# A plan that holds its side steps: `HOLD` in the tracing order of a two-layer decoder step

## The chip, the cores and the metric

The kernel runs on one core of a Trainium2 chip. The metric is device time in microseconds (us) of one execution. Of the kernel before there are three runs: 3317.22, 3322.49 and 3330.22 us, median 3322.49.

## The reference

The reference is one inference step of a decoder trunk with two layers, for a prompt of 2048 tokens and for 8 sampled sequences of 8 tokens each (64 rows), with a model width of 1024. Every layer computes x + W_out(mixer(RMSNorm(x) W_in) * silu(gate)).

- Layer A is a gated DeltaNet with 8 heads of 128. q, k and v go through a causal convolution of width 4 and silu, q and k are normalised per head. Per chunk of tokens a unit lower triangular system is solved (a delta rule in its chunked form), and a state of 128 x 128 per head goes from chunk to chunk: `u = sol_v - sol_k S`, `o = e^G q S + (q k^T * decay) u`, `S' = e^G_last S + k^T u`.
- Layer B is a retention with 4 heads of 256 x 512, rotary positions and a decaying state: `o = (q k^T * D) v + q_dec * q S`, `S' = s_dec S + (k * k_dec)^T v`.

A last RMSNorm follows. Returned are the outputs for prompt and samples, and all states after the step. Everything is computed to float32 accuracy.

## The kernel before

The prompt is cut into four blocks of 512 tokens (`TB`); the 64 sample rows ride with one of the blocks, whose projections are then 576 wide. Layer A goes over the blocks n = 0 to 3 and in each over four groups of two heads (g = 0 to 3); then layer B goes over the blocks and its four heads.

*Projections.* A projection (`proj`, `colproj`, `colproj2`) multiplies a column tile of weights with the normalised block. Weights and activations are split into a high and a low part of type fp32r (`wload`, `split`), and three of the four products are taken (`PASSES`), so a column tile of 512 tokens is 8 x 3 = 24 products of 128 x 512. After each k, which is three products or six, the projection calls `pipe.pump()`. Per group of layer A there are eight such tiles: two of K, two of Z for the group before (`z_proj`), two of Q, two of V. `outproj_A` multiplies the outputs of a pair of groups with W_out.

*Side work.* All that is not a projection is written as Python generators, which `_Pipe` traces step by step in between. Per group of layer A these are

- `front_k` (prio 3): decay matrices, two steps of transposes of K (`tp`), and K K^T (`kp`) with its mask
- `front_x` (prio 2): the inverse of the triangular system. DVE substitutes within 32 x 32 pieces for a long time (`LAT_SUB`), with a way through DRAM before and behind; then PE joins the pieces in four steps of small products (`p1` to `p4`, in the trace `p`)
- `front_q` and `front_v` (prio 4): transposes of Q (`tq`), K Q^T (`kq`), transposes of V (`tv`)
- `chain` (prio 0): the recurrence over four chunks, three steps each (`kyd` and `o` in the trace; the copy `y` at L612 is in the middle of a chunk)
- a post per chunk (`gdn_post`, prio 1): transposes of the output (`oT`), the gate, and the split into `OG`

In blocks 1 and 2 a group of samples is added behind group 0: its fronts, and `chain_s` (prio 1), over four pairs of heads, with five `yield`s each (3.0, `LAT_C`, `LAT_C`, 1.0, 1.0). In layer B `ret_prompt` and `ret_sample` have prio 0, their posts prio 1, `colsum`, `final` and `final_s` prio 2. `gates` of layer A, once a block, has prio 0.

*What sets the order.* `_Pipe` keeps a clock of its own, `t`, which only PE's products advance: 0.4167 ns a column for fp32r, 1.667 ns a column for float32 but at least 0.11 us, 0.11 us a transpose (`mm`, `tr`). A task is runnable when its `deps` are done, and due when `ready <= t`. A step runs the generator to its next `yield`, whose value is the latency after which the task is due again, counted from the start of the step:

```
k.ready = self.t + next(k.gen)
```

`pump` runs all that is due, lowest prio first, until nothing is. `wait(task)` pumps until the task is done, and where nothing is due it moves the clock on to the next `ready`. A task that is added gets its `ready` at that moment, so one that has to wait for its `deps` is due at once when they are done. The latencies are the constants at the end (`LAT_T` 0.8, `LAT_K` 5.5, `LAT_SUB` 51, `LAT_M` 1.8, `LAT_Q` 0.7, `LAT_C` 2.0, `LAT_O` 4.3, `LAT_E` 4.0). The framework makes the queues of the engines from the traced order and inserts all semaphores; with `PIN = False` the traced order is a priority, and an instruction whose operands or buffers are not ready by its own reckoning can be passed by a later one.

*What waits for what.* `front_k` of a group waits for `front_q` of the group before; `front_q` waits for `front_k` and for the last chain added; `front_v` for `front_q`; a chain for `front_v`, `front_x` and the chain before it. The chain of samples stands in this line as well: `front_q` and the chain of group 1 wait for it. Group g begins with `pipe.wait` on the chain of group g - 2, its V projection waits for `front_v` of group g - 1, and `z_proj` for the chain before. `ring` gives the three `OG` buffers out; where the next one is still in use it calls `flush_A(0)`, which waits for the chains and posts of a pair and traces `outproj_A`. This falls on the end of V of group 0 (waiting for the last chain of the block before) and of group 2 (waiting for the chain of group 1) in blocks 1 and 2. Before layer B's V projection of its first head, `open_B` calls `finish_A`, which waits for the last chain and traces the last `outproj_A`.

Weights go through two raw buffers (`wraw`) and three split ones (`w`). PSUM has three banks for projections (`pp`), two for transposes and fronts (`f`), one for the chain (`c`), two for outputs (`o`). All loads and stores are issued by SP in one queue.

Of the kernel before, what the change touches and what calls it, by code (L numbers as in the profile page):

```python
# [35 lines left out]
class _Pipe:  # L36


    def __init__(self, tc):
        self.tc = tc  # L40
        self.t = 0.0
        self.tasks = []
# [17 lines left out]
            k.done = True  # L60
            self.tasks.remove(k)

    def pump(self):
        while True:
            c = [k for k in self._runnable() if k.ready <= self.t]
            if not c:
                return
            self._step(min(c, key=lambda k: (k.prio, k.ready)))

    def wait(self, *ks):  # L70
        for k in ks:
            while k is not None and not k.done:
                self.pump()
                if not k.done:
                    self.t = max(self.t, min(x.ready for x in self._runnable()))

# [11 lines left out]
def tile_hybrid(ctx: ExitStack, tc: tile.TileContext, a: dict, S: int):  # L88
# [7 lines left out]
    def mm(out, lhsT, rhs, start=True, stop=True):  # L96
        ins = nc.tensor.matmul(out, lhsT, rhs, start=start, stop=stop)  # L97
        n = rhs.free_size()
        pipe.t += (max(0.4167 * n, 107.0) if rhs.dtype == F32R else max(1.667 * n, 110.0)) / 1000.0
        if PIN:  # L100
            tc.keep_in_program_order(ins)
        return ins

    def tr(out, x):
        p = x.shape[0]
        ins = nc.tensor.transpose(out, x, ident[:p, :p])  # L106
        pipe.t += 0.11
        if PIN:
            tc.keep_in_program_order(ins)
# [412 lines left out]
    def front_q(x):  # L522
        QK, dec, Gb, kds = x.QK, x.dec, x.Gb, x.kds
        Am = pa.tile([128, 8, 128], F32, tag="Am", name="Am")
        Kd = x.Kd
        eq = pa.tile([128, 8], F32, tag="eq", bufs=2, name="eq")
        for q in range(2):
            tp = v3(pf("tq"), 128)
            for u in range(4):
                tr(tp[:, u, :], QK[:, 4 * q + u, 1, :])  # L530
            for u in range(4):
                ACT.activation(Am[:, 4 * q + u, :], tp[:, u, :], AF.Square, accum_out=eq[:, 4 * q + u : 4 * q + u + 1])
            yield LAT_T
        V.tensor_scalar(eq, eq, EPS, 128.0 * EPS, op0=ALU.add, op1=ALU.mult)
        for q in range(2):
            q4 = slice(4 * q, 4 * q + 4)
            kp = v3(pf("kq"), 128)
            for u in range(4):
                mm(kp[:, u], QK[:, 4 * q + u, 0, :], QK[:, 4 * q + u, 1, :])
            V.tensor_tensor(Am[:, q4], kp, dec[:, q4], op=ALU.mult)  # L540
            V.tensor_tensor(Kd[:, q4], Kd[:, q4], kds[:, q4].unsqueeze(2).to_broadcast([128, 4, 128]), op=ALU.mult)
            yield LAT_Q
            V.tensor_tensor(QK[:, q4, 1, :], QK[:, q4, 1, :], Gb[:, q4], op=ALU.mult)
        x.Am, x.eq = Am, eq

    def front_v(x, VTq):
        vn = pa.tile([128, 8, 128], F32, tag="vn", name="vn")
        for q in range(2):
            q4 = slice(4 * q, 4 * q + 4)
            VTu = VTq(q)  # L550
            if x.samp:
                yield 2.0
            tp = v3(pf("tv"), 128)
            for u in range(4):
                tr(tp[:, u, :], VTu(u))
            V.tensor_tensor(vn[:, q4], tp, x.nk[:, q4].unsqueeze(2).to_broadcast([128, 4, 128]), op=ALU.mult)
            yield LAT_T
        x.vn = vn
# [253 lines left out]
    def add_front(x, gt, nq, hsl, samp):  # L812
        x.fk = pipe.add(front_k(x, gt, nq, hsl, samp), 3, [x.g, last["fq"]], LAT_E, hp=HP_K)
        x.fx = pipe.add(front_x(x, samp), 2, [x.fk, last["fx"]], hp=HP_X)
        last["fx"] = x.fx

    def add_fq(x):
        x.fq = pipe.add(front_q(x), 4, [x.fk, last["ch"]], LAT_E, hp=HP_Q)
        last["fq"] = x.fq
# [47 lines left out]
    for n in range(NB):  # L867
# [22 lines left out]
        for g in range(4):  # L890
# [27 lines left out]
            for hh in range(2):  # L918
                pst = colproj(a["w_in_a"][16 + 2 * g + hh], xk, width)
                if g in (1, 2) and n + 1 < NB:  # L920
                    stats_A(n + 1, [2 * g - 2 + hh])
                    if g == 2 and hh == 1:
# [3 lines left out]
            x.fv = pipe.add(front_v(x, lambda q, VT=VT: lambda u: VT[:, u % 2, (2 * q + u // 2) * 128 : (2 * q + u // 2 + 1) * 128]),  # L926
                            4, [x.fq], LAT_E)
            if g == 3:
# [419 lines left out]


PIN = False  # L1350
LAT_E = 4.0
LAT_SUB = 51.0
LAT_K = 5.5
# [123 lines left out]
```

## Time and profile before

| | |
|---|---|
| median of three runs | 3322.49 us (3317.22 to 3330.22) |
| profiled execution | 3320.32 us, span 3318.5 us |
| granted TensorE clock, mean | 0.995 |
| PE busy | 97% (18847 instructions) |
| weight loads on PE (PEld) | 81% |
| DVE, ACT, POOL busy | 66%, 44%, 7% |
| chain that ended last | PE 83%, DVE 6%, DMA 4%, ACT 3% |

Busy times of PE are those of pipelined instructions: a product of 128 x 512 shows some 0.36 to 0.4 us, while in an unbroken run one starts every 0.23 us. So the distance from start to start tells what a stretch costs, and the busy share only where PE stood still. Layer A takes the time to about 1453 us, layer B the rest.

### The profile page before, as it was taken

The page shows a single profiled execution, that of the slowest core. Times are in us where ns is not written, and L with a number is a line of the kernel's source. Part 1 is how long each engine was busy: PE and PEld are TensorE (multiplying, and loading weights), DVE is VectorE, ACT ScalarE, POOL GpSimd, SP SyncE. Part 2 cuts the span into 40 slices and gives each one's busy share as a digit, 9 for nine tenths or more (in the row PEclk, how much of TensorE's full clock was granted, in tenths as well). Part 3 has the DMA queues.
Part 4 walks back from the last instruction along what each step waited for, and adds up shares of the span by engine and source line. Part 5 has one row for each costly group of instructions (what it writes and reads, how often), then busy time and mean ns, then how long its engine had stood idle before and what let it go on. Part 6 is the DMA issues. An engine that isn't in the chain of part 4 may idle for free.

```text
span 3318.5 us, 50681 instructions
## 1 busy us (share of the span) xinstructions
PE 3231.2 (97%) x18847; PEld 2700.4 (81%) x18847; DVE 2198.3 (66%) x4943; ACT 1453.5 (44%) x3243; POOL 240.2 (7%) x501
## 2 busy tenths in 40 slices
PE   7999999999999999999999999999999999999998
PEld 7999787778788888788888788877888788878886
DVE  6876778688878877755555665556564656575556
ACT  7655555465545645333333442343342433343333
POOL 1221011001110000000000000000000000000000
PEclk9999999999999999999999999999999999999999
DMA  4333454435444343552223442126232523253222
GB/s 134 96 101 85 144 167 142 132 106 152 130 129 126 89 143 99 151 162 82 74 82 106 129 163 89 59 83 194 77 116 82 171 68 116 71 175 117 89 77 70
DMA packets 241111, 379.78 MB, mean 114 GB/s; under 512 B 100688, under 2 KB 130144, under 8 KB 240864
## 3 DMA queue, kind: packets, MB, share of 16 engines
q1 hardware_dynamic: 240864, 376.54, 37.6%
q8 instruction: 148, 2.42, 0.3%
q14 instruction: 99, 0.81, 0.1%
HBM read 318.90 MB, written 55.46 MB: 113 GB/s over the span
## 4 chain that ended last, share of the span: by engine, by line
PE 83%; DVE 6%; DMA 4%; ACT 3%; POOL 1%; issue 1%; SPq 0%; DVEq 0%; POOLq 0%; ACTq 0%
PE pp L97 53%; PE pv L97 10%; PE o L97 5%; PE p L97 5%; PE kyd L97 2%; PE oT L106 1%; DMA st<-in_state_ret 1%; PE kp L97 1%; DVE w L182 1%; PE ap L97 1%; POOL so L572 1%; PE kq L97 1%; PE os L97 1%; ACT on L569 1%; PE pvs L97 1%
## 5 line engine op out<-in xcount | busy, mean ns | idle before, releaser
L97 PE MATMUL pp<-xn,w 128*128 128x512 f32 (+1 forms) x7760 | 1648.5, 362 | 13.2 <-ACT w L181 4.2
L97 PEld LDWEIGHTS pp<-xn,w 128*128 128x128 f32 x7760 | 1267.3, 189 | 210.2 <-issue 13.9
L181 ACT CAST w<-wraw 128x1024 fp32r<-128x1024 f32 x416 | 436.8, 1050 | 691.4 <-PE pp L97 449.0
L182 DVE TENSOR_TENSOR w<-wraw,w 128x1024 fp32r<-128x1024 f32 x416 | 508.4, 1222 | 249.1 <-ACT w L181 248.0
L97 PE MATMUL pp<-OG,w 128*128 128x512 f32 (+1 forms) x2880 | 582.6, 360 | 6.3 <-DVE xas L1167 3.2
L97 PEld LDWEIGHTS pp<-OG,w 128*128 128x128 f32 x2880 | 482.0, 190 | 89.8 <-issue 3.6
L97 PE MATMUL pv<-w,xn 128*128 128x512 f32 x1536 | 370.8, 396 | 0.0
L97 PEld LDWEIGHTS pv<-w,xn 128*128 128x128 f32 x1536 | 287.1, 188 | 73.8 <-issue 5.0
L1162 DVE TENSOR_TENSOR xa<-xa,pp 128x512 f32<-128x512 f32 (+2 forms) x160 | 90.2, 579 | 137.2 <-PE pp L97 137.1
L728 DVE SCALAR_TENSOR_TENSOR acc<-pp,cw,acc 128x511 f32<-128x511 f32 (+2 forms) x216 | 160.4, 742 | 22.0 <-ACT acc L725 21.7
L990 POOL TENSOR_TENSOR so<-oss,rsc 128x1 f32<-128x1 f32 x72 | 17.8, 247 | 1412.5 <-ACT on L988 1412.5
L981 DVE TENSOR_TENSOR rt<-pp,cs 128x512 f32<-128x512 f32 (+2 forms) x80 | 46.3, 578 | 105.9 <-PE pp L97 105.9
L473 DVE TENSOR_TENSOR VP<-VP,tm 128x66 f32<-128x66 f32 (+26 forms) x510 | 106.5, 209 | 4.4
L471 DVE TENSOR_TENSOR tm<-LP,VP 128x66 f32<-128x66 f32 (+26 forms) x510 | 104.3, 204 | 4.4
L97 PE MATMUL p<-Vt,Kt 128*128 128x512 f32 x384 | 104.4, 405 | 0.6 <-ACT on L992 0.6
L195 ACT CAST OG<-og 128x256 fp32r<-128x256 f32 x192 | 71.7, 405 | 62.0 <-DVE og L628 33.4
L97 PE MATMUL o<-Sc,Qc 128*128 128x512 f32 x360 | 93.4, 394 | 0.0
L196 DVE TENSOR_TENSOR OG<-og,OG 128x256 fp32r<-128x256 f32 x192 | 75.4, 420 | 20.8 <-ACT OG L195 20.5
L106 PE MATMUL oT<-ident,on 128*128 128x128 f32 x432 | 73.1, 276 | 11.4 <-DVE on L573 9.5
L97 PEld LDWEIGHTS p<-Vt,Kt 128*128 128x128 f32 x384 | 68.2, 189 | 13.0 <-ACT on L992 0.9
L106 PEld LDWEIGHTS oT<-ident,on 128*128 128x128 f32 x432 | 52.6, 140 | 31.9 <-DVE on L573 14.6
L97 PEld LDWEIGHTS o<-Sc,Qc 128*128 128x128 f32 x360 | 66.6, 188 | 14.4
(369 smaller groups left out, 3947.3 us busy)
## 6 DMA issues: line engine op xcount, KB each, us to landing
wraw<-in_w_in_a SPq DMA_DIRECT2D x128, 512.0 KB, 3.7
wraw<-in_w_qkg SPq DMA_DIRECT2D x128, 512.0 KB, 3.6
wraw<-in_w_v SPq DMA_DIRECT2D x64, 512.0 KB, 3.7
wraw<-in_w_out_b SPq DMA_DIRECT2D x64, 512.0 KB, 3.6
wraw<-in_w_out_a SPq DMA_DIRECT2D x32, 512.0 KB, 3.7
st<-in_state_ret SPq DMA_DIRECT2D x64, 256.0 KB, 3.6
out_ret_s<-st SPq DMA_DIRECT2D x64, 256.0 KB, 2.7
LP<-sl SPq DMA_DIRECT2D x72, 128.0 KB, 2.9
```

The source lines that it names most:

```text
L97: ins = nc.tensor.matmul(out, lhsT, rhs, start=start, stop=stop)
L106: ins = nc.tensor.transpose(out, x, ident[:p, :p])
L181: ACT.copy(w[:, 0, :], raw)
L182: V.tensor_tensor(w[:, 1, :], raw, w[:, 0, :].bitcast(F32), op=ALU.subtract)
L195: ACT.copy(hi, x)
L196: V.tensor_tensor(lo, x, hi.bitcast(F32), op=ALU.subtract)
L471: V.tensor_tensor(tv, LP[:, m, m + 1 : m + 1 + n].unsqueeze(2).to_broadcast([128, n, ncol]), VP[:, m, 0:ncol].unsqueeze(1).to_broadcast([1 ...
L473: V.tensor_tensor(VP[:, m + 1 : m + 1 + n, 0:ncol], VP[:, m + 1 : m + 1 + n, 0:ncol], tv, op=ALU.subtract)
L569: ACT.activation(on[:, j, :], o[:, j, :], AF.Square, scale=128.0 ** -0.5, accum_out=ss[:, j : j + 1])
L728: V.scalar_tensor_tensor(acc[:, sh:], ap[:, : TB - sh], cw[:, ct, j : j + 1], acc[:, sh:], op0=ALU.mult, op1=ALU.add)
L981: V.tensor_tensor(t[1], p1, f1[:, s:e], op=ALU.mult)
L1162: V.tensor_tensor(xa[:, ct, s:e], xa[:, ct, s:e], p, op=ALU.add)
```

## The change

`pump` gets a parameter `hold`. With it, and where no due task has prio 0 and none has been due for `HOLD` (6.0 us on the plan's clock) or longer, it returns without a step. Once one such task is found, the rest of that call runs all that is due, as before. Projections call `pump()` and so hold; `wait` calls `pump(False)`. The empty lines in the class are all else that differs.

```
 class _Pipe:
...
-    def pump(self):
+    def pump(self, hold=True):
         while True:
             c = [k for k in self._runnable() if k.ready <= self.t]
-            if not c:
+            if not c or hold and not any(k.prio == 0 or k.ready + HOLD <= self.t for k in c):
                 return
+            hold = False
             self._step(min(c, key=lambda k: (k.prio, k.ready)))
 
     def wait(self, *ks):
         for k in ks:
             while k is not None and not k.done:
-                self.pump()
+                self.pump(False)
                 if not k.done:
                     self.t = max(self.t, min(x.ready for x in self._runnable()))
...
 PIN = False
+HOLD = 6.0
 LAT_E = 4.0
 LAT_SUB = 51.0
```

## Rows read from the trace of the kernel before

**Rows 1.** The page's busy times: engine, busy us, share of the span, instructions.

```profile
PE 3231.2 (97%) x18847; PEld 2700.4 (81%) x18847; DVE 2198.3 (66%) x4943; ACT 1453.5 (44%) x3243; POOL 240.2 (7%) x501
```

**Rows 2.** Stages: start:end, length, busy us by engine, granted clock, DMA share, GB/s.

```profile
40.00:1430.00 1390.00, 1354.78 (x9393) 1148.38 (x9392) 1081.82 (x3058) 753.46 (x1969) 168.24 (x327) 0.99 0.43 123
430.00:771.00 341.00, 326.75 (x2175) 263.93 (x2173) 269.83 (x763) 182.62 (x486) 36.67 (x77) 0.99 0.44 127
612.00:630.00 18.00, 18.00 (x78) 14.40 (x77) 14.34 (x42) 3.79 (x4) 0.00 (x0) 1.00 0.72 224
1490.00:3318.00 1828.00, 1795.80 (x9065) 1483.99 (x9063) 1059.36 (x1802) 664.48 (x1221) 66.26 (x156) 1.00 0.33 104
```

**Rows 3.** PE in order of time, block 1: start, us, line, operation, tiles, count.

```profile
546.20 1.40 PE L97 MATMUL pp<-xn,w 128*128 128x512 f32 x5
547.45 0.61 PE L97 MATMUL o<-y,Am 128*128 128x128 f32 x4
547.81 0.94 PE L97 MATMUL pp<-xn,w 128*128 128x512 f32 x3
548.59 1.02 PE L97 MATMUL dss<-ye,Kd 128*128 128x512 f32 x2
```

**Rows 4.** PE in order of time, from layer A to layer B.

```profile
1434.37 19.01 PE L97 MATMUL pp<-xn,w 128*128 128x512 f32 x81
1453.22 22.40 PE L97 MATMUL pp<-OG,w 128*128 128x512 f32 x96
```

**Rows 5.** PE in order of time, two places of front_x's products.

```profile
635.61 0.69 PE L97 MATMUL p<-VD,X 32*32 32x32 f32 x16
636.23 0.97 PE L97 MATMUL pp<-xn,w 128*128 128x512 f32 x3
...
1225.73 1.09 PE L97 MATMUL p<-VD,X 32*32 32x32 f32 x32
1226.76 0.97 PE L97 MATMUL pp<-xn,w 128*128 128x512 f32 x3
```

**Rows 6.** ACT in order of time: the first and last of four copies in chain_s.

```profile
513.67 0.37 ACT L694 COPY y<-kyd 128x256 f32<-128x256 f32 x1
...
546.53 0.37 ACT L694 COPY y<-kyd 128x256 f32<-128x256 f32 x1 [5.14 <-PE kyd L97]
```

**Rows 7.** DVE and ACT in order of time, around the samples' blocks.

```profile
510.53 1.28 DVE L447 TENSOR_TENSOR X<-kp,dec 128x512 f32<-128x512 f32 x2
...
587.66 0.37 ACT L612 COPY y<-kyd 128x256 f32<-128x256 f32 x1
...
862.66 1.28 DVE L447 TENSOR_TENSOR X<-kp,dec 128x512 f32<-128x512 f32 x2
...
939.85 0.37 ACT L612 COPY y<-kyd 128x256 f32<-128x256 f32 x1 [0.38 <-PE kyd L97]
```

**Rows 8.** Stages: the stretch before an output projection of block 1.

```profile
593.00:612.00 19.00, 13.53 (x97) 11.18 (x97) 14.94 (x60) 6.71 (x36) 2.73 (x6) 1.00 0.01 3
```

**Rows 9.** PE in order of time, block 2's first output projection.

```profile
768.10 0.44 PE L106 MATMUL oT<-ident,on 128*128 128x128 f32 x2 [0.16 <-DVE Am L540]
...
769.78 2.47 PE L97 MATMUL pp<-OG,w 128*128 128x512 f32 x10
```

**Rows 10.** Waits of SP's queue: line, waited for, us in total, times, longest.

```profile
SPq L180 <- DVE w L182: 1562.9, 279, 22.1
```

**Rows 11.** Stages: ten microseconds at the end of chain_s.

```profile
550.00:555.00 5.00, 2.20 (x10) 1.24 (x9) 2.82 (x11) 2.20 (x8) 1.83 (x3) 0.96 0.44 145
555.00:560.00 5.00, 5.00 (x28) 4.37 (x27) 4.05 (x15) 2.57 (x17) 0.00 (x0) 0.69 0.41 120
```

**Rows 12.** PE in order of time, an output projection's products inside a chain.

```profile
587.38 0.93 PE L97 MATMUL pp<-OG,w 128*128 128x512 f32 x3
```

**Rows 13.** Groups of PE by form, 40 to 1430 us: busy, mean ns, idle before.

```profile
L106 PE MATMUL oT<-ident,on 128*128 128x128 f32 x142 | 29.3, 283 | 11.1 <-DVE on L573 9.5 <-DVE Am L540 0.8 <-DVE nd L371 0.5
L97 PE MATMUL dss<-ye,Kd 128*128 128x512 f32 x32 | 17.2, 618 | 4.2 <-DVE S L710 4.2
```

More of the change, by code (lines that the diff above doesn't have):

```diff
@@ L61, in _step, with pump @@
             self.tasks.remove(k)
-    def pump(self):
+    def pump(self, hold=True):
         while True:
             c = [k for k in self._runnable() if k.ready <= self.t]
-            if not c:
+            if not c or hold and not any(k.prio == 0 or k.ready + HOLD <= self.t for k in c):
                 return
+            hold = False
             self._step(min(c, key=lambda k: (k.prio, k.ready)))
@@ L72, in wait @@
             while k is not None and not k.done:
-                self.pump()
+                self.pump(False)
                 if not k.done:
@@ L1350 @@
 PIN = False
+HOLD = 6.0
 LAT_E = 4.0
```

## The prediction

> **What bounds the kernel now.** I read the page's busy times first. The reader is to see that TensorE (PE) is busy 97% of the span [rows 1]: time is gained only by giving PE fewer or shorter gaps and lost by giving it new ones. The table by stage comes second, because the change acts on steps that stand between projections, and these differ between the halves. In layer A after the opening, 40 to 1430 us, PE is busy 1354.78 of 1390.00 us, so 35.2 us are idle; in layer B, 1490 to 3318 us, 32.2 of 1828.00 [rows 2]. B has few steps off its chain (the posts, `final`, `colsum`), and its chain step comes due 4.2 us after the last (6.0 once in a sample step), or polls every 0.3 us, so a post waits there for little. I put B at nothing, with 2 us either way, and all that follows is about layer A.
>
> Third I read PE's own order of instructions, to price one interruption. Five projection products take 547.45 - 546.20 = 1.25 us from start to next start, three take 548.59 - 547.81 = 0.78 us, and the four chain products between them 0.36 us [rows 3]. In an unbroken run 81 products take 1453.22 - 1434.37 = 18.85 us, 0.233 each [rows 4]. So the two pieces of projection are 0.08 us each over 5 x 0.233 and 3 x 0.233. Even if nothing of this is given back in the chain products, entering a side step costs some 0.08 us. One kind is dearer: 16 products on 32x32 pieces of `front_x` take 636.23 - 635.61 = 0.62 us alone, where 32 of them joined take 1226.76 - 1225.73 = 1.03 us [rows 5]. Joining two halves saves 0.21 us on their own rows; with the projection product that is late on entering, I call it 0.3 us (an estimate).
>
> **The change part by part.** `pump` gets a condition: where no due step has prio 0, and none has been due for 6 us of the plan's clock, it returns without a step. Prio 0 are `chain`, `gates` and layer B's retention; the posts and `chain_s` have 1, `front_x` 2, `front_k` 3, `front_q` and `front_v` 4. `wait` calls `pump(False)` and works as before. No product, copy or DMA is added or removed; steps move.
>
> *What joins.* While a prompt chain lives, it has three steps for each of four chunks, with 2.0 us between steps, so a side step is held about 2 us and then goes beside a chain step. Per group there are some 17 side steps that put work on PE (3 of `front_k`, 4 of `front_x`, 4 of `front_q`, 2 of `front_v`, 4 posts). About six of them, the posts and a part of `front_k`, fall in a chain's life: 16 groups x 6 x 0.08 = 7.7 us at best. I take 5 us of it. The halves of `front_x` may join as well, 16 groups x 2 x 0.3 = 9.6 us, of which I take 3. Together -8 us. The bound on this side is all idle of A, -35 us; on the other it is 0, since the interruptions may stay as many as they are.
>
> *What is late where no chain lives.* There a side step is alone, and holding it joins it to nothing: it comes 6 us later at each `yield`. A step whose own products advance the plan's clock beyond its next latency goes on in the same pump: `kq` (4 products of 128 columns at 1.667 ns a column, 0.85 us, against 0.7), the second part of `front_x` (24 products at 0.11, 2.6 us, against 1.8). The others wait. `front_x` so gets up to three holds, 18 us, and `front_k` up to five, 30 us, less where two tasks share a release. What counts is whether a wait ends on them, so I went to the places where projections stand behind a chain directly.
>
> *The sample chains* (blocks 1 and 2). `chain_s` has prio 1 and is itself held. Its copies `y` stand at 513.67 and, three head pairs later, 546.53 us, 11.0 us a pair [rows 6]. Four of the five yields of a pair wait 6 us more (after the query step its 16 products advance the clock 3.4 us against 2.0), so a pair comes to 11 + 24 = 35 us. The next group's `front_q` and chain wait for `chain_s`, and the next `wait` on them lets all run unheld, so not 4 x 24 us are lost. The chain of the next group begins now when `front_x` is ready: `kp` is masked at 510.53 and the chain's first `y` is at 587.66; in block 2 masking is at 862.66 and the first `y` at 939.85 [rows 7]. Between the end of the prompt chain and that `kp` lie four holds: two in `front_q`, after each of its transposes, and two in `front_k`, whose transposes go in one release with those of `front_v`. That is 24 us, less some 6 that the nine yields there lose now to the pump's own grain (three products, 0.7 us): `kp` comes about 17 us later. The solve behind it is unchanged, so the chain would start 17 us later, and `outproj_A` of that pair, which stands directly behind it, as well. The projections of V that PE can do meanwhile are done anyway and only swap places. Bounds: 0, if PE takes the steps at their old time, and 35 us, if a whole pair of samples is left uncovered. I take 12 us for each of the two blocks, nearer to 17 than to 0: the chain runs almost uncovered even now, with 5.5 idle of the 19 us from 593 on [rows 8], so PE has little else to take. Sum +24.
>
> *Block 1 to 2.* The last transpose of a post is at 768.10 and the first output product at 769.78 [rows 9]: 1.7 us of slack between the last chain of block 1 and the projections that wait for it. Two holds in its `front_x` are 12 us, less 1.7 and less what its neighbours release early: I take +8, bounds 0 and 18.
>
> *Layer A to B.* From 1434.37 on, after the last post, 81 projection products run before the output projection at 1453.22 [rows 4]: 18.9 us of slack. The last group's `front_x` can be 18 us late and its `front_k` some 10 (no chain lives while it runs): 28 - 19 = 9, taken as +8, bounds 0 and 29.
>
> *DMAs.* The moved steps issue theirs on SP's queue (`Gb`, the solve's way through DRAM, the samples' states). SP stands 1562.9 us in total in front of weight loads, for a buffer [rows 10]; a load that is traced later is behind more of these, as long as one projection each. That is a part of the lateness above, and not counted again. POOL gets no more work.
>
> Sum: -8 + 24 + 8 + 8 = +32 us on the profiled execution's 3320.32 us: 3352 us. The median shown is 2.2 us above that execution, inside the runs' own spread, and is not added.
>
> A gap of PE costs more than its length: after one that leaves PE busy only 2.20 of 5 us from 550 on, the granted clock of the next 5 us is 0.69, the lower level for a part of them [rows 11]; (1 - 0.69) x 5 = 1.6 us. The Trainium skill's page "TensorE: Matmul & The Clock Gate" (section "Why this matters for your kernels") warns of idle gaps between bursts of products, after which the clock falls to half; the trace agrees. Four such gaps would add 6.4 us, which I leave to the range.
>
> **The rivals.** *No change.* The plan's order is a preference, and PE may reach a held step early when a projection is not ready, or the lateness falls into slack. For it: output products run at 587.38 us before this chain has ended, which they stand behind in the plan, so PE does fill [rows 12]; the slack before layer B is 19 us. Against it: the slack of 1.7 us, and that the chain in 593 to 612 is almost uncovered. With the three late terms at a quarter, +10, and -8: 3322.
>
> *Faster.* Steps that PE reaches before their operands are ready are, when held, ready on arrival. Idle before the transposes of posts is 11.1 us in A and before `dss` 4.2 [rows 13]; with the 9.6 us of joined halves that is 24.9, and at four fifths of it, -20: 3300. It decides if the late chains stay within their slack and most of those waits are of steps that a hold reaches. For it: these waits are PE's largest after the opening. Against it: most of the posts' waits lie in uncovered chains, where `wait` doesn't hold. The Trainium skill's page "Perfetto Trace Analysis" (section "Identifying the Most-Contended Engine") says that headroom on PE is judged by the busy share of weight loads, not of products. By that measure an unbroken stretch of projections has 14.40 of 18.00 us, 80%, and 430 to 771 us has 77% [rows 2], which leaves 3% of 341, about 10 us (an estimate) and would give 3310.
>
> *Late everywhere.* The chain of a group is needed before the group after next begins. If 48 us of holds (30 + 18) outrun the slack in each of some 14 groups by 6 us, +84 less 8: 3396. Against it: releases are shared, and a group has about 87 us (1390 / 16).
>
> *The change does not do what it says*, because the steps stay single: that is the premise of my sum where no chain lives, and it costs time, not nothing.
>
> **How the numbers follow.** My forecast 0.46, no change 0.27, faster 0.16, late everywhere 0.11. The forecast's own range is 3328 to 3375. A measurement tells 0.5%, 16.6 us, from no change, so from 3306 to 3339 is the same. Of the forecast's 0.46, 0.06 lies below 3339; of no change 0.03 below 3306; of the faster rival 0.03 above it. Faster 0.16, same 0.33, slower 0.51. The range takes in the faster rival's centre and the rival of late chains: 3298 to 3398.
>
> **What would show it.** Right: the four sample `y` copies of a block lie more than 15 us apart at first; the chain that now begins at 587.66 begins over 600; PE is idle for more than 10 us before the output projections near 615, 770 and 1455; PE's idle in A rises from 35 to over 55 us. Wrong: that idle falls, or the `y` copies keep 11 us. If the pieces of projection become longer and A shorter, the price of an interruption was what mattered.

## The result and the profile after

The changed kernel takes 3376.94 us (median of five runs, 3376.06 to 3379.0); the kernel before takes 3321.2 beside it (3317.22 to 3330.22). The ratio is 1.017 with an interval of [1.0156, 1.0184]: slower by 55.7 us. The profiled execution has a span of 3376.0 us, 57.5 more than before.

The page's busy times of the kernel after (engine, busy us, share, instructions) answer to [rows 1].

```profile
PE 3253.9 (96%) x18847; PEld 2718.3 (81%) x18847; DVE 2216.4 (66%) x4943; ACT 1446.4 (43%) x3238; POOL 243.6 (7%) x501
```

The instructions of PE are the same, 18847, and PE's busy time has grown by 22.7 us only; so 34.8 of the 57.5 us are time in which PE stands still. The busy share of weight loads is 81% in both kernels, though one is 57.5 us longer: it does not show this loss.

The next two fences are tables by stage, of the kernel before and of the kernel after, cut at the same events of the program: the starts of the output projections behind the chain of group 1 in block 1 and behind block 1, the ends of the one behind block 1 and of the one behind the chain of group 1 in block 2, the start of the one that ends layer A, and the first and last products of V in layer B (`pv`). Columns: start:end, length, busy us and instructions of PE, PEld, DVE, ACT and POOL, granted clock, DMA share, GB/s. The last two lines of the first fence are a place in layer B, those of the second two stretches with a low clock and the 40 us ahead of layer A's last output projection.

```profile
40.00:611.66 571.66, 549.69 (x4055) 483.52 (x4053) 439.77 (x1260) 330.64 (x893) 91.79 (x190) 0.99 0.41 116
611.66:769.78 158.12, 155.28 (x991) 127.50 (x988) 124.09 (x336) 85.08 (x215) 11.54 (x20) 1.00 0.42 125
792.90:987.27 194.37, 189.06 (x1345) 153.53 (x1344) 154.77 (x459) 95.67 (x270) 28.18 (x59) 1.00 0.47 130
987.27:1453.22 465.95, 460.84 (x3007) 383.87 (x3006) 352.04 (x959) 237.44 (x583) 36.40 (x60) 1.00 0.41 120
...
1475.50:3237.80 1762.30, 1743.59 (x8827) 1442.13 (x8826) 1014.68 (x1725) 640.49 (x1173) 62.83 (x148) 1.00 0.34 108
...
2300.00:2306.00 6.00, 2.21 (x11) 1.45 (x10) 6.00 (x10) 2.07 (x4) 0.00 (x0) 0.97 0.43 132
2306.00:2310.00 4.00, 4.00 (x21) 4.00 (x22) 2.02 (x5) 0.30 (x1) 0.00 (x0) 0.61 0.79 223
```

```profile
40.00:634.73 594.73, 558.65 (x4056) 489.08 (x4054) 447.50 (x1255) 325.25 (x890) 100.21 (x190) 0.97 0.39 112
634.73:807.25 172.52, 164.17 (x1020) 134.03 (x1018) 128.73 (x344) 88.44 (x220) 12.34 (x20) 0.99 0.40 118
825.40:1047.87 222.47, 199.95 (x1341) 164.01 (x1340) 162.50 (x476) 100.00 (x273) 27.89 (x59) 0.94 0.42 117
1047.87:1518.43 470.56, 461.34 (x3007) 385.12 (x3005) 354.35 (x958) 231.61 (x578) 33.80 (x60) 1.00 0.42 118
...
1540.70:3295.90 1755.20, 1742.20 (x8826) 1440.14 (x8825) 1015.84 (x1725) 639.94 (x1173) 60.08 (x148) 1.00 0.34 108
...
597.10:614.20 17.10, 14.84 (x140) 12.76 (x138) 6.10 (x14) 4.57 (x13) 1.19 (x3) 0.50 0.16 39
986.20:1003.30 17.10, 13.18 (x134) 11.96 (x135) 7.17 (x16) 5.10 (x11) 0.30 (x1) 0.50 0.22 52
...
1478.43:1518.43 40.00, 40.00 (x205) 33.63 (x203) 22.44 (x39) 13.92 (x30) 2.67 (x6) 1.00 0.36 112
```

From these rows the 57.5 us can be put in places. (In block 1 the output projection ends at 792.9 before and 825.4 after, 32.5 later; its start moved by more, 37.5, because 18 of its products run ahead at 787.30.)

| place | predicted | measured | how |
|---|---|---|---|
| to the output projection of block 1's group 1 | -8 + 12 | +23.1 | 634.73 - 611.66 |
| from there to the end of block 1 | +8 | +9.4 | 32.5 - 23.1 |
| block 2, through the output projection of its group 1 | +12 | +28.1 | 222.47 - 194.37 |
| the rest of block 2 and block 3, to layer A's last output projection | +8 | +4.6 | 470.56 - 465.95 |
| layer B, between its products of V | 0 | -7.1 | 1755.20 - 1762.30 |
| the rest, at the end | 0 | -0.6 | 57.5 less the others |
| **sum** | **+32** | **+57.5** | |

The -8 of the prediction was meant for all groups of layer A; it stands in the first row for want of a place.

Layer A is 65.2 us longer. Length less busy time gives PE's idle: 14.1, 5.5, 17.2 and 4.1 us more in the four stretches of A, 40.9 in all. In the other 24.3 PE is busy longer over the same products. For that look at the clock: in block 2's stretch it falls from 1.00 to 0.94. Its length grew 10.9 us beyond its idle time (28.1 - 17.2), and 0.06 x 222.47 = 13.3 is the most that such a mean can take. The half level itself, 1.2 GHz, shows in the two stretches of 17.1 us at 0.50. In all, by the trace's own record of the clock, it is granted for 64.9 us of layer A after and for 17.1 before; half of the difference, 23.9 us, is the most that the clock can have cost. How much of the 24.3 it did cost isn't shown, since products that wait for each other also count as busy.

Now the events themselves. In order of time on DVE, the mask of `kp` of group 1 in blocks 1 and 2, which answers to the first lines of [rows 7].

```profile
537.77 0.69 DVE L451 TENSOR_TENSOR X<-kp,dec 128x512 f32<-128x512 f32 x1 [0.88 <-PE kp L101]
...
928.76 0.69 DVE L451 TENSOR_TENSOR X<-kp,dec 128x512 f32<-128x512 f32 x1 [0.28 <-PE kp L101]
```

On ACT, the four copies `y` of `chain_s` in block 1 [rows 6], then the first and last `y` of the chain of group 1 and the first one in block 2 [rows 7].

```profile
543.06 0.37 ACT L698 COPY y<-kyd 128x256 f32<-128x256 f32 x1 [0.39 <-PE kyd L101]
552.62 0.37 ACT L698 COPY y<-kyd 128x256 f32<-128x256 f32 x1 [1.84 <-PE kyd L101]
567.41 0.37 ACT L698 COPY y<-kyd 128x256 f32<-128x256 f32 x1 [6.49 <-DVE tm L475]
576.85 0.37 ACT L698 COPY y<-kyd 128x256 f32<-128x256 f32 x1 [7.05 <-PE kyd L101]
...
609.64 0.37 ACT L616 COPY y<-kyd 128x256 f32<-128x256 f32 x1 [1.41 <-PE kyd L101]
...
626.10 0.37 ACT L616 COPY y<-kyd 128x256 f32<-128x256 f32 x1 [2.74 <-PE kyd L101]
...
1001.06 0.37 ACT L616 COPY y<-kyd 128x256 f32<-128x256 f32 x1 [1.41 <-PE kyd L101]
```

On PE, one step of `front_x` in the low stretch, the output projections behind the two chains [rows 9], and the end of layer A [rows 4].

```profile
602.95 1.97 PE L101 MATMUL p<-VD,X 64*64 64x64 f32 x16 [0.46 <-ACT X L511]
...
634.73 19.90 PE L101 MATMUL pp<-OG,w 128*128 128x512 f32 x78
...
805.28 0.38 PE L110 MATMUL oT<-ident,on 128*128 128x128 f32 x2
807.25 18.30 PE L101 MATMUL pp<-OG,w 128*128 128x512 f32 x78
...
1515.45 0.38 PE L110 MATMUL oT<-ident,on 128*128 128x128 f32 x2
1515.59 3.00 PE L101 MATMUL pp<-xn,w 128*128 128x512 f32 x12
1518.43 22.40 PE L101 MATMUL pp<-OG,w 128*128 128x512 f32 x96
```

The reader is to see one delay going down a line of waits. In block 1 `kp` is 27.2 us later than before, the chain's first `y` 22.0, its last 23.1 (603.0 before), and the projection behind it 23.1. In block 2 `kp` is 66.1 later, of which 32.5 were there at the end of block 1's output projection: 33.6 of its own, of which 28.1 arrive at the end of the projection behind the chain.

### The profile page after: what moved, and what is told of

It reads as the page before. It is cut to its first block, busy times and chain, and to the rows that moved or that the text cites. A ratio compares the mean times of both kernels' runs of the same rounds, so it can differ in the third digit from the quotient of the medians.

```text
span 3376.0 us, 50653 instructions
## 1 busy us (share of the span) xinstructions
PE 3253.9 (96%) x18847; PEld 2718.3 (81%) x18847; DVE 2216.4 (66%) x4943; ACT 1446.4 (43%) x3238; POOL 243.6 (7%) x501
## 4 chain that ended last, share of the span: by engine, by line
PE 62%; DVE 3%; DMA 2%; ACT 1%; issue 1%; POOL 1%; SPq 0%; DVEq 0%; POOLq 0%; ACTq 0%
PE pp L101 39%; PE pv L101 10%; PE o L101 4%; PE p L101 3%; PE oT L110 1%; DMA st<-in_state_ret 1%; PE kyd L101 1%; PE ap L101 1%; DMA out_ret_s<-st 1%; PE pvs L101 1%; PE os L101 1%; PE kT L110 0%; DVE acc L732 0%; PE ps L101 0%; ACT w L185 0%
## 5 line engine op out<-in xcount | busy, mean ns | idle before, releaser
L101 PE MATMUL pp<-xn,w 128*128 128x512 f32 (+2 forms) x7760 | 1620.8, 361 | 15.8 <-ACT xn L199 4.6
L101 PEld LDWEIGHTS pp<-xn,w 128*128 128x128 f32 (+1 forms) x7760 | 1274.9, 189 | 219.9 <-issue 10.1
L1262 DVE TENSOR_SCALAR GT<-GT,onB 128x512 f32<-128x512 f32 x64 | 31.1, 486 | 82.1 <-ACT GT L1261 81.2
L1261 ACT ACTIVATE GT<-pp 128x512 f32<-128x512 f32 (+1 forms) x80 | 39.4, 514 | 98.7 <-PE pp L101 98.7
```

The source lines that it names most:

```text
L1261: ACT.activation(GT[:, d, s:e], p, AF.Silu)
```

## The experiments

The theory: what costs the time is that `front_q`, `front_k` and `front_x` are late at the two places where projections stand directly behind a chain whose cover the samples have used up. Its rivals: that `chain_s`, itself held, makes the next chain late; that the loss is spread over all groups; and that the held posts cost, or bring, what is seen. Besides, the price of an interruption was to be tested by itself. Times are medians; a difference is to the kernel before run beside it (3324.8 for e1, e2, e4 and e5; 3324.7 for e3, e6, e8 and e9; 3326.7 for e7, e10 and e11).

### Where: holding off, or on, around the samples alone

`on` lets `pump` hold only where it is set; the stretch goes from the adding of the samples to the adding of group 2's chain, in blocks 1 and 2.

```
+            if not c or hold and self.on and not any(...):
...
+                pipe.on = False      # e4 (it starts True); True in e5 (it starts False)
                 sample_qkv(s, y)
...
+            if g == 2:
+                pipe.on = True       # e4; False in e5
```

> The changed kernel, but nothing is held from the moment the samples are added (blocks 1 and 2, after group 0) to the end of group 2 of the same block; elsewhere steps are held as in the change. Theory S (the 56 us are lost where the samples' fronts and chain_s stand between two chains): the two stretches come back to what they were, the time falls to 3321 to 3335. Rival R (holds are late in every group, the samples are only where it shows first): most of the loss stays, 3355 to 3377.

> The opposite: steps are held only between the adding of the samples and the end of group 2 in blocks 1 and 2, nowhere else. Theory S: nearly the whole loss is there, 3365 to 3380. Rival R: 3325 to 3345. If both parts are independent, the loss here and that of the run with holds everywhere else add up to 56 us.

Not held there: 3334.05, ratio 1.0028 [1.0016, 1.0039], +9.3. Held there alone: 3384.07, 1.0189 [1.0171, 1.0206], +59.3. So the place is right: groups 1 and 2 and the samples of blocks 1 and 2 hold most of the loss, and a hold there alone makes all of it (and 4 us more than the range that was expected). The two do not add up: without layer B's 7 us, which e4 has and e5 has not, they are 16.3 + 59.3 = 75.6 against 62.8 for the whole change in A. Why holding elsewhere takes 13 us off what is lost here was not tested.

### Who: the samples' chain, or the fronts

```
+                y.ch.free = True                                    # e1: chain_s opens the pump
-            ... any(k.prio == 0 or k.ready + HOLD <= self.t ...)
+            ... any(k.prio == 0 or k.free or k.ready + HOLD <= self.t ...)   # e1
+            ... any(k.prio != 1 or k.ready + HOLD <= self.t ...)             # e2: all fronts open it
```

> The changed kernel, but a due step of the samples' chain opens the pump as a prompt chain's does; fronts and posts are held as before. Theory Y (the lateness is that of the samples' chain, which is held at four of five yields of a pair): the time falls to 3325 to 3340. Theory F (the fronts are late: kp of group 1 is 29 us later than in the kernel before, and front_x, on which the next chain waits, with it): the chain still begins near 607, the time stays at 3360 to 3377, because the samples' chain has only moved beside projections and the output projection still waits for the chain.

> The changed kernel, but a due step of any front opens the pump (prio 2 to 4, and prio 0); only posts and the samples' chain can be held, until one of these is due. Theory F: fronts are back at their old times, 3321 to 3340. Theory Y: the samples' chain is still alone for most of its life and held, 3355 to 3377.

With `chain_s` free: 3376.62, ratio 1.0164 [1.0149, 1.0179]; nothing is won. With the fronts free: 3336.56, 1.0037 [1.0022, 1.0051]. The same events as above, e1 first (DVE, then ACT, in order of time), then e2.

```profile
538.45 0.69 DVE L452 TENSOR_TENSOR X<-kp,dec 128x512 f32<-128x512 f32 x1 [0.94 <-PE kp L102]
...
543.92 0.36 ACT L699 COPY y<-kyd 128x256 f32<-128x256 f32 x1
...
577.84 0.37 ACT L699 COPY y<-kyd 128x256 f32<-128x256 f32 x1 [7.06 <-PE kyd L102]
...
610.92 0.37 ACT L617 COPY y<-kyd 128x256 f32<-128x256 f32 x1 [1.41 <-PE kyd L102]
```

```profile
505.27 1.28 DVE L451 TENSOR_TENSOR X<-kp,dec 128x512 f32<-128x512 f32 x2
...
516.74 0.37 ACT L698 COPY y<-kyd 128x256 f32<-128x256 f32 x1 [0.70 <-PE kyd L101]
544.59 0.37 ACT L698 COPY y<-kyd 128x256 f32<-128x256 f32 x1 [3.20 <-PE kyd L101]
...
581.36 0.35 ACT L616 COPY y<-kyd 128x256 f32<-128x256 f32 x1
```

In e1 every event stays where the whole change has it: freeing `chain_s` moves nothing. By the time it runs the program already stands in a `wait`, which does not hold: the last product of Q of group 2 starts at 537.1 there, ahead of all four `y`. In e2 `kp` is back on time, and there the samples' chain shows the slow pair that the prediction worked out as 35 us: 27.9 us from the first `y` to the second (26.3 in e8 below, where `front_x` alone of the fronts is held). Even so the chain of group 1 isn't late in block 1, where it begins at 581.36; in block 2 it begins at 946.5, 6.7 later than before. So holding the samples' chain costs something only where the fronts are on time, and not through a late chain of group 1 in block 1: in its trace e2 is 1.3 us behind at the last product of block 1's output projection (793.9) and 24.6 behind at layer A's last output projection (1477.84). Where those arise wasn't followed up.

### Only the posts held

This is e2's condition with e1's flag: `k.prio != 1 or k.free or k.ready + HOLD <= self.t`.

> Only posts are held (a due step of the chain, a front or the samples' chain opens the pump). This takes the lateness away and leaves some 60 to 130 joined interruptions. At the price of 0.08 us for each that the prediction took, 5 to 10 us faster than the kernel before, 3311 to 3317; if a joined interruption saves next to nothing, 3319 to 3326.

3314.6, ratio 0.998 [0.9966, 0.9994]. The time lies in the range that was expected at 0.08 us for each joined interruption, but not for that reason. Layer A is nearly as before: the first product of V in layer B stands at 1471.9 (1475.5 before). Counted in the traces, the projections of A are interrupted 466 times, 468 before: holding a post joins it to next to nothing. Most of the gain is layer B's, which takes 1755.5 us between its products of V (1762.3 before). Against e2, whose one difference is that `chain_s` is held as well, this is 11.8 + 10.1 = 21.9 us: the price of holding the samples' chain where the fronts are on time.

### Which front

```
+            ... any(k.prio in (0, 3, 4) or ...)   # e8: front_k, front_q, front_v open the pump
+            ... any(k.prio in (0, 2) or ...)      # e9: front_x opens it
```

> The changed kernel, but a due step of front_k, front_q or front_v opens the pump (as chain and gates do); front_x, the posts and the samples' chain are held. Theory F1 (what is lost is the lateness of front_q and front_k, so that kp of group 1 and with it the solve begin some 29 us late): kp is back near 510 us in block 1, the next chain begins before 592, the time is 3325 to 3345. Rival F2 (the holds inside front_x, between its joining steps, make the chain late): 3360 to 3377.

> The changed kernel, but a due step of front_x opens the pump; front_k, front_q, front_v, the posts and the samples' chain are held. Theory F1: kp of group 1 is still near 538 us and its chain begins near 605, the time is 3360 to 3377. Rival F2: 3325 to 3345.

`kp` of group 1 in block 1, in order of time on DVE, e8 and then e9.

```profile
516.05 0.68 DVE L451 TENSOR_TENSOR X<-kp,dec 128x512 f32<-128x512 f32 x1
```

```profile
535.59 0.69 DVE L451 TENSOR_TENSOR X<-kp,dec 128x512 f32<-128x512 f32 x1 [1.00 <-PE kp L101]
```

With `front_k`, `front_q` and `front_v` free: 3347.05, 1.0077 [1.0059, 1.0096], 2 us over the expected range, `kp` 5.5 us late and the chain's first `y` at 595.4, where it was to be before 592. With only `front_x` free: 3373.87, 1.0158 [1.0142, 1.0174], `kp` still 25.1 late. So the three short fronts carry most: freeing them takes +55.7 to +22.4. `front_x` held costs another 22.4 - 11.8 = 10.6 once these are on time, and only 55.7 - 49.2 = 6.5 while they are late.

### Late fronts without any holding

The kernel before with one number changed: the latency behind which `front_k` of group 1 goes on to `kp`, in blocks 1 and 2.

```
-        yield LAT_K
+        yield LAT_K + (0.0 if samp else x.late)
+            x.late = 26.0 if n in (1, 2) and g == 1 else 0.0
```

> The kernel before, with nothing held at all; only kp of group 1 in blocks 1 and 2 comes 26 us of the plan's clock later (two steps in the whole program). Theory F1, sufficiency: late kp alone makes solve, joining, chain and output projection late: the chain begins near 608 instead of 588 us, and 35 to 50 us are lost in all, 3355 to 3375. Rival (the loss needs the holding of the other steps as well, above all the samples' chain that runs without projections beside it): kp's lateness is covered by the samples' chain and the projections of V, at most 20 us, 3320 to 3342.

3362.88, ratio 1.0109 [1.0089, 1.0129], +36.2. The events on DVE, ACT and PE in order of time:

```profile
530.42 0.69 DVE L447 TENSOR_TENSOR X<-kp,dec 128x512 f32<-128x512 f32 x1
...
598.18 0.37 ACT L612 COPY y<-kyd 128x256 f32<-128x256 f32 x1 [1.41 <-PE kyd L97]
...
624.39 18.46 PE L97 MATMUL pp<-OG,w 128*128 128x512 f32 x78
```

Two late steps, with nothing held, make 36 of the 56 us: lateness alone makes most of the loss. `kp` comes 19.9 us after that of [rows 7] and the output projection 12.7 after its own. (The profiled run of before has `kp` some 5 us late itself: PE's clock is 0.85 from 300 to 345 us there, and in a run with the same order in A, e6 below, it is 1.00 and `kp` stands at 505.2. Against that one, `kp` is 25 later, as set.) The other 20 us, and how they divide between late solves and the chain before, stay open.

### How much: HOLD of 2 and of 12

> The changed kernel with HOLD 2.0 instead of 6.0. Theory F1: each hold is a third, kp of group 1 is some 9 us late instead of 27, and the loss about a third or less, since some of it falls into slack: 3322 to 3342. Rival (what is lost is the order, not the time held): 3355 to 3377.

> The changed kernel with HOLD 12.0. Theory F1: kp grows later, but from the place where group 2 waits for front_v nothing is held, which bounds it; also the slack at the other places is used up: 3385 to 3425. Rival (the loss is bounded already at 6): 3370 to 3382.

2 us: 3340.74, 1.004 [1.0026, 1.0054]. 12 us: 3426.96, 1.0299 [1.0282, 1.0316]. `kp` on DVE, with 2 and then with 12:

```profile
517.19 0.69 DVE L451 TENSOR_TENSOR X<-kp,dec 128x512 f32<-128x512 f32 x1
```

```profile
560.41 1.28 DVE L451 TENSOR_TENSOR X<-kp,dec 128x512 f32<-128x512 f32 x2
```

`kp` is 6.7, 27.2 and 49.9 us late with 2, 6 and 12, and the kernel 14.0, 55.7 and 100.3 slower (the last 2 us over the expected range). From 2 to 6 the loss grows by 2.0 us for each us of lateness of this one `kp` (41.7 for 20.5), from 6 to 12 again by 2.0 (44.6 for 22.7): it goes with the time held, as the theory has it, and isn't a price of the changed order. That the first microseconds cost as much isn't shown. Against the `kp` at 505.2 the three are 12.0, 32.6 and 55.2 late, and the same line starts at some 5 us of lateness. Nor is it shown that the factor of 2 is one for each of the two blocks, since the hold moves other steps too.

### The price of an interruption

The kernel before, pumping after every second k instead of after each (the same line in `colproj2`).

```
-            if k < nk - 1:
+            if k < nk - 1 and k % 2:
                 pipe.pump()
```

> The kernel before, with the pump called after every second k of a projection instead of every one, so side steps meet at half as many places and come 0.35 us later on average. It prices an interruption by itself: at 0.08 us for each of some 100 to 150 that fall away 8 to 12 us faster, 3310 to 3316; if a switch costs next to nothing, 3318 to 3330.

3317.24, ratio 0.9972 [0.996, 0.9985]. That lies between the two ranges that were expected and by itself decides neither. In the traces the interruptions of projections in A fall from 468 to 416, but layer B's first product of V stands at 1477.6, 2.1 us later than before: nothing is won in A. What is won in the trace is in layer B, 1757.7 us between its products of V against 1762.3. (The two profiled executions differ by 3.1 us, the medians by 9.5; the rest isn't located.)

The trace of before says why. Where a projection goes on after a side step, its second product starts 0.085 us late (the median of all such places in A with two products or more), as the prediction had read it. But the last product of the side step has been followed after 0.03 us, where it is followed after 0.11 by another of its kind. The next lines, of PE after the change, show it: from 786.49 to 786.94 four products take 0.45 us, and from 786.94 to the projection at 787.30 four take 0.36.

```profile
786.49 0.61 PE L101 MATMUL kyd<-y,Kd 128*128 128x128 f32 x4
786.94 0.61 PE L101 MATMUL o<-y,Am 128*128 128x128 f32 x4
787.30 4.08 PE L101 MATMUL pp<-OG,w 128*128 128x512 f32 x15
```

So 0.08 of the 0.085 us are given back, and some 0.01 us is left of the price of an interruption (an estimate from these medians, which leaves out waits inside the side steps).

### Holding in layer B alone

`self.on` as above, False at first, True after layer A:

```
         finish_A()
+        pipe.on = True
```

> Steps are held in layer B alone, from the last output projection of layer A on; layer A is traced as in the kernel before. Between the first and the last V projection of layer B the changed kernel took 7 us less than the kernel before. If that comes from holding in B, this kernel is 5 to 8 us faster than before, 3313 to 3318; if it hung on the state in which A leaves the buffers, within 2 us of it.

3313.1, ratio 0.9973 [0.996, 0.9986], faster than both kernels. Its layer B:

```profile
1473.20:3229.40 1756.20, 1743.53 (x8826) 1439.56 (x8825) 1015.21 (x1725) 640.09 (x1173) 60.26 (x148) 1.00 0.34 108
```

1756.20 us against 1762.30 before. In all kernels here, B's stretch is 1762.3 to 1765.1 where it is traced as before (before, e5, e10) and 1754.6 to 1756.2 where it is held for 2 or 6 us; with 12 us it is 1762.9. Most of it comes from one place. On PE in order of time, before and then after, at the same step of the program:

```profile
2300.35 1.09 PE L97 MATMUL p<-Vt,Kt 128*128 128x512 f32 x4
...
2304.68 0.50 PE L97 MATMUL pp<-OG,w 128*128 128x288 f32 x2 [3.25 <-DVE xas L1167]
```

```profile
2365.67 0.40 PE L101 MATMUL p<-Vt,Kt 128*128 128x512 f32 x1
2366.45 5.73 PE L101 MATMUL pp<-OG,w 128*128 128x288 f32 x41 [0.38 <-DVE xas L1171]
```

Before, an output projection that starts waits 3.25 us for DVE to add the one before it (`xas`), and the stretch 2306 to 2310 that follows has a clock of 0.61 (first fence of the section above). Held, that wait is 0.38 us. One wait of PE for DVE went; it wasn't the interruptions that got cheaper. In e3, where nothing but posts is held, it is 0.38 us as well (at 2297.20): held posts are enough to free it. Which of them does wasn't tried.

## Why the prediction was right, and where it was not

**The sign, the main place and the mechanism were right.** Most of the loss is where it was put, behind the two sample chains, as e4 and e5 show, and comes from late fronts, as e2 and e10 show. Its size was not: +32 forecast, +57.5 in the profiled execution, and 3376.94 us lies 2 above the forecast's own range of 3328 to 3375. The chain that began at 587.66 begins at 609.64, over 600 as foretold, and PE's idle in A is 76.2 us (40.9 more), over 55. Layer B's answer holds within the 7 us told below; that DMAs need no term of their own wasn't tested.

**The term of the sample chains was mis-sized:** 12 us a block, measured 23.1 and 28.1. Two numbers of its working failed. `kp` was to be 17 us late, from four holds behind the prompt chain; it is 27.2 late. The way from that chain to `kp` gives 15 of them; the other 12.3 were there already, since the chain of group 0 itself ends late (its last `y` moves from 490.5 to 502.8). Either kind of its fronts does that alone: with `front_x` free (e9) that `y` is at 505.6, with the three others free (e8) at 498.6, with all free (e2) at 485.2, as in e6. The prediction had counted lateness of that kind for the end of block 1 and for layer B, but not here. And then 12 of 17 was taken, as if nearly a third of the wait were covered. Little covers it: 23.1 of 27.2 arrive at the projection in block 1, 28.1 of 33.6 in block 2. The row that it was read from, 5.5 us idle of 19 [rows 8], was the sign of that: a chain that runs bare has no cover left for a later start.

**The bonus for joined interruptions was wrong:** -8 us, measured nothing. It took 0.08 us an interruption and left open whether the chain products give some of it back. They do: the four in [rows 3] take 0.36 us, where four of their kind take 0.45, and some 0.01 us is left. The count did fall, from 468 to 335, but 133 x 0.01 is 1 us. The other part, the joined halves of `front_x`, did not come: 32 of these products stand in one run five times in either trace. e3 shows besides that a held post joins to next to nothing in A, and e11 that fewer interruptions alone bring nothing there. A held post didn't find its operand ready either: PE's wait for the output `on` of a post has doubled. The waits of before and of after (line, waited for, us in total, times, longest):

```profile
PE oT L106 <- DVE on L573: 9.5, 15, 1.5
```

```profile
PE oT L110 <- DVE on L577: 18.3, 25, 1.4
```

The faster rival had taken the opposite for granted, that a held step finds its operands ready.

**Two signs did not come.** One is the idle time in front of the projections, told below. The `y` of `chain_s` were to lie more than 15 us apart at first; they are 9.6, 14.8 and 9.4 apart, 11.3 on average, where before it was 11.0. The prediction had named that, copies that keep 11 us, as a sign of being wrong, and for this part it was: that `chain_s` is itself held costs nothing in the whole change (e1). The chain is so late that it runs in the `wait` and not beside projections. e2 shows the foretold spacing, 27.9 us, where the fronts don't hold it up.

**The two smaller places** came out near their terms, +9.4 for +8 and +4.6 for +8, the second by luck. The foretold idle time of more than 10 us in front of each of the three projections did not show: it is 9.4, 4.9 and 0 us in the 40 us before 634.73, 807.25 and 1518.43. At the end of layer A the late steps stay within the slack: 12 products, 2.8 us, still run between the last post at 1515.45 and 1518.43, of the 18.9 before. The 4.1 us of idle in that last stretch lie in the rest of block 2, where PE's idle grew from 2.4 to 6.4 us; by what, wasn't followed up.

**Layer B** was put at 0 with 2 us either way and brought 7: the wait at 2300 was not looked for.

**The clock** was left to the range, with four gaps of 1.6 us. Here it should have been a term of the sum: of the 65.2 us of layer A, 24.3 are PE busy for longer, and up to 23.9 can be the clock's. The Trainium skill's page "TensorE: Matmul & The Clock Gate" (section "Why this matters for your kernels") says that idle gaps between bursts of products throw the clock back to half; the trace agrees, with 0.50 in two stretches of 17.1 us behind gaps: PE was busy 4.16 of the 7 us from 590 on and 3.35 of the 6 us from 980 on.

## What to carry to other kernels

Holding a step to join it with another pays only if another comes due soon; a step that stands alone at each of its yields is late by the hold at each of them, and a task with five yields by up to five holds. Price such a change at the wait that ends on the held task, not at the engine's average: "off the chain" here were exactly the steps that the next chain waits for. And where a chain already runs uncovered, take its lateness at nearly its full price, here 23.1 of 27.2 us.

## What the runs showed of the hardware

PE's clock stayed at its half level for 17.1 us while PE was busy 14.84 of them, mostly with small products that depend on each other (32 x 32 and 64 x 64 pieces, and 128 x 128 in float32). The same 16 products on 64 x 64 pieces took 1.97 us there, and in the trace of before, at full clock:

```profile
641.25 1.14 PE L97 MATMUL p<-VD,X 64*64 64x64 f32 x16
```

So a chain that is left alone on PE is not only uncovered; here a part of it also ran at the half level. The four `y` of the late chain lie 16.5 us apart from first to last (609.64 to 626.10), against 15.3 before (587.66 to 603.0), for the same work.

An interruption of fp32r products of 128 x 512 by a few float32 products of 128 columns costs next to nothing, some 0.01 us (an estimate): the projection's second product comes 0.085 us late, but its first has started 0.03 us after the last of the others, which otherwise start every 0.11.
